# Two sequence layers on one core: every fourth low part of the weights is subtracted by GpSimd

## The chip, the cores and the metric

One core of a Trainium2 chip runs the whole kernel. The time is the device time in microseconds (us); before and after are compared by medians of several runs. A profiled execution gives the trace from which all rows below come. The engines are TensorE (PE, its weight loads as PEld), VectorE (DVE), ScalarE (ACT), GpSimd (POOL) and SyncE (SP), which here only issues transfers.

## The reference

Two layers are computed for 256 tokens of width 2048, in float32, the first one's output (after a norm) feeding the second.

```python
h = _rmsnorm(x, norm_gain);  u = h @ w_in            # first layer
o_a = fox attention (8 heads of 128) * silu(z_a)     # causal softmax with forget gates
o_b = rwkv7 scan (16 heads of 64), group norm, * silu(z_b)
m = sigmoid(g_a) * (o_a @ w_proj_fox) + sigmoid(g_b) * (o_b @ w_proj_rwkv)
x = _rmsnorm(x + m @ w_out, final_norm_gain)
...
proj = rms_norm(x, norm_g) @ w_in                    # second layer
o_conv = (gated causal convolution) @ w_conv_out
o_mla  = (latent attention, 16 heads, rope) @ w_mla_out
o_mem  = (attention to 256 memory tokens) @ w_mem_out
x = x + (sigmoid(g_conv)*o_conv + sigmoid(g_mla)*o_mla + sigmoid(g_mem)*o_mem) @ w_o
```

Nearly all arithmetic is the product of 256 tokens with some 84 million weights.

## The kernel before, in words

The weights lie in memory packed into 658 blocks of 128 x 1024 floats, in the order in which the matrix products (`gemm`) use them. TensorE multiplies in a float32 form of lower precision (`F32R`), so each operand is split into a high part (a copy in that form) and a low part (the operand less its high part), and each product is three matmuls: high by high, high by low, low by high.

`conv_to` prepares a block. `dma_to` loads it into a `raw` buffer (SP's queue, L402); ScalarE copies it to `whi` (`acopy`, L278 in the profile); VectorE subtracts that from `raw` to give `wlo` (`sub`, which goes through the helper `tt`, L241). There are four buffers each of `raw`, `whi` and `wlo` (`NRAW`, `NHI`), and `gemm` asks for blocks three ahead of the one that it multiplies (`AHEAD`). `wlo` of a block must be done before its `raw` buffer is loaded again; `whi` and `wlo` of a block must be read by TensorE before the block four later is written there. Block i = 0 is done in two halves; the first twelve blocks are taken in an order of their own (`block_at`).

All else (norms, attention, the scan, splitting activations, moving results out) is written as "side jobs": Python generators whose steps `pump` issues between the matmuls of `gemm`. A planner decides how many. It keeps a clock for TensorE, VectorE and ScalarE; each helper (`mm`, `tt`, `ts`, `stt`, `act`) adds the cost that it expects of its instruction, `CD + n / 960` us for `tt`. `busy()` stops the issue of steps while VectorE's or ScalarE's clock is more than a margin (1.5 us) ahead of TensorE's, and a step is not followed by the next one of its job before the result is expected. `finish` issues what is left of a job at once, where a later product needs it. The written order gives priorities; the framework then lays down the order in each engine's queue by when it expects an instruction's inputs, so that fills or loads with free buffers can stand far ahead of their place in the text. On each engine the queue is then run in order.

GpSimd's queue holds, before the change, only fills and the issue of transfers: in `head_rs` (L663 to L665: a row of norms to memory, `hd`, and back spread over partitions, `hr`), in `rwkv_job` (L879, L995 `Ld`, L1002 to L1006, L1020 to L1027 `Xd`, `Yd`, `XA`, `YF`), in `conv_job` (L1546 to L1550), and loads of `mt`, `fg`, `xr`, `xbd`, `xo`.

Of the kernel before, what the change touches and what calls it, by code (L numbers as in the profile page):

```python
# [10 lines left out]
F32 = mybir.dt.float32  # L11
# [3 lines left out]
ALU = mybir.AluOpType  # L15
# [211 lines left out]
def hybrid_kernel(ctx: ExitStack, tc: tile.TileContext, io, out):  # L227
    nc = tc.nc
# [10 lines left out]
    def tt(o, a, b, op):  # L239
        clock["dve"] += CD + fsz(o) / 960.0  # L240
        DVE.tensor_tensor(out=o, in0=a, in1=b, op=op)  # L241
# [7 lines left out]
    def sub(o, a, b):  # L249
        tt(o, a, b, ALU.subtract)  # L250
# [29 lines left out]
    def acopy(o, a, scale=1.0):  # L280
        act(o, a, AF.Copy, scale=scale)
# [18 lines left out]
    def nm(s):  # L300
        serial[0] += 1
        return f"{s}_{serial[0]}"
# [69 lines left out]
    groups, nblk = weight_groups()  # L372
    byname = {e["name"]: e for e in groups}
    st = {"dma": 0, "conv": 0}
    raw_t, hi_t, lo_t = {}, {}, {}

    def block_at(i):

        if i >= 12:
            return i  # L380
        return 4 + 2 * (i // 3) + i % 3 - 1 if i % 3 else i // 3

    def half(p):
        return slice(512 * p, 512 * p + 512)

    def dma_to(n):
        while st["dma"] < min(n, nblk):
            i = st["dma"]
            j = block_at(i)
            raw_t[j] = wpool.tile([128, 1024], F32, name=nm("raw"), tag="raw", bufs=NRAW)  # L390
            x = i // 3
            if i == 0:
                for p in range(2):
                    nc.scalar.dma_start(out=xt[0][:, 2 * p:2 * p + 2, :], in_=io["xT"][:, 2 * p:2 * p + 2, :])
                    nc.sync.dma_start(out=raw_t[j][:, half(p)], in_=io["W"][j, :, half(p)])
            else:
                if i % 3 == 0 and x < 4:
                    nc.sync.dma_start(out=xt[x], in_=io["xT"][:, 4 * x:4 * x + 4, :])
                if i == 12:
                    nc.sync.dma_start(out=lw2f[0:96, :], in_=io["w2"])  # L400
                    nc.sync.dma_start(out=la2f[0:96, :], in_=io["a2"])
                nc.sync.dma_start(out=raw_t[j], in_=io["W"][j])  # L402
            st["dma"] += 1

    def conv_to(n):
        while st["conv"] < min(n, nblk):
            i = st["conv"]
            j = block_at(i)
            dma_to(i + 1)
            hi_t[j] = wpool.tile([128, 1024], F32R, name=nm("whi"), tag="hi", bufs=NHI)  # L410
            lo_t[j] = wpool.tile([128, 1024], F32R, name=nm("wlo"), tag="lo", bufs=NHI)
            for p in ([half(0), half(1)] if i == 0 else [slice(0, 1024)]):
                acopy(hi_t[j][:, p], raw_t[j][:, p])
                sub(lo_t[j][:, p], raw_t[j][:, p], hi_t[j][:, p].bitcast(F32))
            del raw_t[j]
            st["conv"] += 1
            dma_to(i + 1 + NRAW)
# [60 lines left out]
    def gemm(name, pairs, evac):  # L478
# [5 lines left out]
        for b0 in range(0, e["nb"], step):  # L484
            bl = list(range(base + b0, base + min(b0 + step, e["nb"])))
            conv_to(bl[-1] + 1)
            conv_to(bl[-1] + 1 + AHEAD)
            ks = [(b, i, (b - base) * per + i) for b in bl for i in range(per)]
            if acc is None:
# [119 lines left out]
    def out_pair(name):  # L609
        return tuple(claim(t) for t in new_pair(name))  # L610
# [107 lines left out]
    def start_tile(i):  # L718

        x = xt[i]  # L720
        p = new_pair("xg")
        xg.append(p)
        for cs in ((range(2), range(2, 4)) if i == 0 else (range(4),)):
            for c in cs:
                acopy(p[0][:, c, :], x[:, c, :], scale=pc("norm_gain", 4 * i + c))
            for c in cs:
                stt(p[1][:, c, :], x[:, c, :], pc("norm_gain", 4 * i + c), p[0].bitcast(F32)[:, c, :], ALU.mult,
                    ALU.subtract)
            if cs[0] == 0:
                conv_to(3 * i + 1)  # L730
# [1026 lines left out]
    for j in range(4):  # L1757
        p = out_pair("ol")
# [10 lines left out]
    for j in range(4):  # L1769
        gemm(f"gl{j}", h2, gate(gt))  # L1770
        p = out_pair("mg")
# [68 lines left out]
```

## Time and profile before

| | |
|---|---|
| median of 3 runs | 2010.94 us (2008.88 to 2014.69) |
| the profiled execution | 2012.98 us, its span 2011.2 us |
| granted TensorE clock | 0.998 |
| busy in the span | TensorE 1996.2, VectorE 1276.6, ScalarE 985.3, GpSimd 61.5 us |
| weights converted | 659 high parts and 659 low parts (658 blocks, one in halves) |
| moved by transfers | 370.86 MB |

How to read it: the span runs from the first to the last instruction. A row of groups gives line, engine and operation, result and operands with their shapes, how often, the busy time and the mean in ns, and the idle time of that engine just ahead, with what ended it. A row of waits gives who waited for whom, the total, how often, and the longest. A row of the timeline gives start and duration in us. Ends of matmuls are modelled, so a busy TensorE may hide short gaps.

### The profile page before, as it was taken

Reading aid. Unit: us, or ns where it says so; the run is one execution under the profiler, and the core shown is the slowest. Engines: PE = TensorE matmul, PEld = TensorE weight load, DVE = VectorE, ACT = ScalarE, POOL = GpSimd, SP = SyncE. Lnnn points to the kernel's source line nnn. Section 1 sums busy time; section 2 is a strip of 40 time slices with the busy share of each in tenths; the row PEclk is TensorE's granted clock in tenths of the full one; section 3 lists DMA queues with packets and bytes.
Section 4 is the critical chain, followed back from the end, with each engine's and each line's share of the span. In section 5 each row is a group of like instructions: output and inputs, shape, how many; then the busy total and the mean of one; then the engine's idle time right before and its main releaser. Section 6 shows DMA issues by size and latency. Waiting matters only on the chain.

```text
span 2011.2 us, 30300 instructions
## 1 busy us (share of the span) xinstructions
PE 1996.2 (99%) x11916; PEld 1736.4 (86%) x11916; DVE 1276.6 (63%) x2039; ACT 985.3 (49%) x1344; POOL 61.5 (3%) x112
## 2 busy tenths in 40 slices
PE   9999999999999999999999999999999999999999
PEld 9999999898877888888898888888888889988887
DVE  8776846878447578666756766657556555555554
ACT  6744445454444545455545545445445444444442
POOL 0002000020100000000000000000000000000000
PEclk9999999999999999999999999999999999999999
DMA  7455544536546766665555554655555555666564
GB/s 271 159 183 162 193 141 138 171 114 202 180 156 223 230 197 203 201 219 190 181 189 184 168 177 154 206 181 191 169 178 188 168 179 179 189 213 212 190 199 146
DMA packets 104190, 370.86 MB, mean 184 GB/s; under 512 B 12466, under 2 KB 13410, under 8 KB 104048
## 3 DMA queue, kind: packets, MB, share of 16 engines
q1 hardware_dynamic: 97136, 350.11, 53.0%
q0 software_dynamic: 6480, 18.21, 3.2%
q8 instruction: 93, 1.52, 0.3%
q10 hardware_dynamic: 432, 0.61, 0.1%
q14 instruction: 49, 0.40, 0.1%
HBM read 361.00 MB, written 5.80 MB: 182 GB/s over the span
## 4 chain that ended last, share of the span: by engine, by line
PE 96%; DVE 2%; DMA 1%; issue 1%; ACT 0%; POOL 0%; SPq 0%; DVEq 0%; POOLq 0%
PE acc.lz L286 5%; PE acc.ga L286 4%; PE acc.gc L286 4%; PE acc.gm L286 4%; PE acc.gl L286 4%; PE acc.wo L286 4%; PE acc.w L286 4%; PE acc.lo L286 4%; PE acc.gb L286 4%; PE acc.fq L286 2%; PE acc.r L286 2%; PE acc.mz L286 2%; PE acc.fk L286 2%; PE acc.zb L286 2%; PE acc.pf L286 2%; PE acc.vr L286 2%
## 5 line engine op out<-in xcount | busy, mean ns | idle before, releaser
L241 DVE TENSOR_TENSOR wlo<-raw,whi 128x1024 fp32r<-128x1024 f32 (+1 forms) x659 | 804.0, 1223 | 615.8 <-ACT whi L278 607.8
L278 ACT ACTIVATE whi<-raw 128x1024 fp32r<-128x1024 f32 (+1 forms) x659 | 696.1, 1058 | 800.9 <-PE acc.lo L286 51.1
L286 PE MATMUL acc.lz<-h2l,whi 128*128 128x256 f32 x256 | 72.3, 283 | 0.0
L286 PE MATMUL acc.lz<-h2h,whi 128*128 128x256 f32 x256 | 72.3, 283 | 0.0
L286 PE MATMUL acc.lz<-h2h,wlo 128*128 128x256 f32 x256 | 72.0, 283 | 0.0
L286 PE MATMUL acc.gb<-wlo,hh 128*128 128x512 f32 x128 | 49.9, 390 | 1.7 <-DVE wlo L241 1.7
L286 PE MATMUL acc.ga<-whi,hl 128*128 128x512 f32 x128 | 50.4, 394 | 0.0
L286 PE MATMUL acc.ga<-wlo,hh 128*128 128x512 f32 x128 | 50.3, 393 | 0.0
L286 PE MATMUL acc.gc<-whi,h2h 128*128 128x512 f32 x128 | 50.2, 393 | 0.0
L286 PE MATMUL acc.gm<-whi,h2h 128*128 128x512 f32 x128 | 50.1, 392 | 0.0
L286 PE MATMUL acc.gl<-wlo,h2h 128*128 128x512 f32 x128 | 50.1, 391 | 0.0
L286 PE MATMUL acc.gm<-whi,h2l 128*128 128x512 f32 x128 | 50.0, 391 | 0.0
L286 PE MATMUL acc.gc<-wlo,h2h 128*128 128x512 f32 x128 | 50.0, 391 | 0.0
L286 PE MATMUL acc.gm<-wlo,h2h 128*128 128x512 f32 x128 | 50.0, 391 | 0.0
L286 PE MATMUL acc.gc<-whi,h2l 128*128 128x512 f32 x128 | 50.0, 390 | 0.0
L286 PE MATMUL acc.ga<-whi,hh 128*128 128x512 f32 x128 | 50.0, 392 | 0.0
L286 PE MATMUL acc.gl<-whi,h2h 128*128 128x512 f32 x128 | 49.9, 391 | 0.0
L286 PE MATMUL acc.w<-wlo,mgh 128*128 128x512 f32 x128 | 49.9, 390 | 0.0
L286 PE MATMUL acc.wo<-wlo,mh 128*128 128x512 f32 x128 | 49.9, 390 | 0.0
L286 PE MATMUL acc.w<-whi,mgh 128*128 128x512 f32 x128 | 49.9, 390 | 0.0
L286 PE MATMUL acc.gl<-whi,h2l 128*128 128x512 f32 x128 | 49.8, 389 | 0.0
L286 PE MATMUL acc.wo<-whi,ml 128*128 128x512 f32 x128 | 49.8, 389 | 0.0
(646 smaller groups left out, 5533.1 us busy)
## 6 DMA issues: line engine op xcount, KB each, us to landing
raw<-in_W SPq DMA_DIRECT2D x657, 512.0 KB, 3.4
hr<-hd POOLq DMA_DIRECT2D x8, 256.0 KB, 4.5
xr<-in_xtm POOLq DMA_DIRECT2D x4, 512.0 KB, 6.1
mt<-in_memT POOLq DMA_DIRECT2D x4, 512.0 KB, 6.5
xbd<-x1g POOLq DMA_DIRECT2D x4, 512.0 KB, 3.7
xo<-xbd POOLq DMA_DIRECT2D x4, 512.0 KB, 4.9
out_tm<-xo SPq DMA_DIRECT2D x8, 256.0 KB, 4.8
xt<-in_xT SPq DMA_DIRECT2D x3, 512.0 KB, 7.6
```

The lines of the kernel that those rows point to most:

```text
L241: DVE.tensor_tensor(out=o, in0=a, in1=b, op=op)
L278: ACT.activation(out=o, in_=a, func=f, scale=scale, **kw)
L286: TE.matmul(o, lhsT=l, rhs=r, start=start, stop=stop)
```

## The change

In `conv_to`, for each block whose number i (in order of conversion) leaves 3 when divided by 4, and which is not among the last 8, the low part is computed by GpSimd's `tensor_tensor` instead of VectorE's. These are 162 of 658 blocks. The operands, the buffers and the place in the text are the same. The helper `sub` is not called for them, so that the planner's VectorE clock is not advanced either, and the planner has no clock for GpSimd.

```diff
             for p in ([half(0), half(1)] if i == 0 else [slice(0, 1024)]):
                 acopy(hi_t[j][:, p], raw_t[j][:, p])
-                sub(lo_t[j][:, p], raw_t[j][:, p], hi_t[j][:, p].bitcast(F32))
+                if i % 4 == 3 and i < nblk - 8:
+                    nc.gpsimd.tensor_tensor(out=lo_t[j][:, p], in0=raw_t[j][:, p], in1=hi_t[j][:, p].bitcast(F32), op=ALU.subtract)
+                else:
+                    sub(lo_t[j][:, p], raw_t[j][:, p], hi_t[j][:, p].bitcast(F32))
             del raw_t[j]
             st["conv"] += 1
             dma_to(i + 1 + NRAW)
```

## The prediction

> **What bounds the kernel now.** I read the page's head first, then TensorE's own waits, then the two groups that make the weights, then one quiet stretch as a timeline, and last everything that GpSimd does.
>
> ```profile
> span 2011.2 us, 30300 instructions
> PE 1996.2 (99%) x11916; PEld 1736.4 (86%) x11916; DVE 1276.6 (63%) x2039; ACT 985.3 (49%) x1344; POOL 61.5 (3%) x112
> PE 96%; DVE 2%; DMA 1%; issue 1%; ACT 0%; POOL 0%; SPq 0%; DVEq 0%; POOLq 0%
> ...
> L241 DVE TENSOR_TENSOR wlo<-raw,whi 128x1024 fp32r<-128x1024 f32 (+1 forms) x659 | 804.0, 1223 | 615.8 <-ACT whi L278 607.8
> ```
>
> TensorE is busy for 1996.2 of 2011.2 us, so 15.0 us are all that any change to another engine could win by those records. VectorE has the low parts as its largest group, 804.0 of its 1276.6 us, and 37% of the span free. The second view, TensorE's waits, says how much of the 15.0 us the low parts cause:
>
> ```profile
> PE acc.vr L286 <- DVE wlo L241: 2.6, 1, 2.6
> PE lora L286 <- ACT xgh L278: 1.7, 1, 1.7
> PE acc.gb L286 <- DVE wlo L241: 1.7, 1, 1.7
> PE acc.fz L286 <- DVE wlo L241: 1.5, 2, 1.0
> PE acc.zb L286 <- DVE wlo L241: 1.1, 2, 0.9
> ```
>
> Four places, 2.6 + 1.7 + 1.5 + 1.1 = 6.9 us, is the whole price of late low parts: 0.34% of the time.
>
> Third, a quiet stretch, as ScalarE (high part), VectorE (low part) and the weight queue do it:
>
> ```profile
> 1858.25 1.06 ACT L278 ACTIVATE whi<-raw 128x1024 fp32r<-128x1024 f32 x1 [1.66 <-PE acc.lo L286]
> 1860.97 1.06 ACT L278 ACTIVATE whi<-raw 128x1024 fp32r<-128x1024 f32 x1 [1.66 <-PE acc.lo L286]
> ...
> 1869.13 1.06 ACT L278 ACTIVATE whi<-raw 128x1024 fp32r<-128x1024 f32 x1 [1.66 <-PE acc.lo L286]
> 1859.35 1.23 DVE L241 TENSOR_TENSOR wlo<-raw,whi 128x1024 fp32r<-128x1024 f32 x1 [1.50 <-ACT whi L278]
> 1860.60 22.09 SPq L402 DMA_DIRECT2D raw<-in_W  x9
> raw<-in_W SPq DMA_DIRECT2D x657, 512.0 KB, 3.4
> ```
>
> The period is 1860.97 - 1858.25 = 2.72 us a block. A high part starts when TensorE has left the block four before it (four buffers), so TensorE still has three blocks, 8.16 us, until it needs this one. The low part is done 1860.58 - 1858.25 = 2.33 us after that start: 5.8 us early. At its end the queue reloads the raw buffer (1860.60, landing 3.4 us later), which is converted four blocks on, at 1869.13; the reload is 1869.13 - 1860.60 - 3.4 = 5.1 us early. These two spares carry the forecast.
>
> **The change, part by part.** The weights have 658 blocks; those with i % 4 == 3 below 650 are i = 3, 7, ... 647, 162 of them. One such low part comes up every 4 x 2.72 = 10.9 us.
>
> *VectorE loses 162 x 1.223 = 198 us.* That is worth something only where TensorE waits for it, the 6.9 us. One block in four moves, and the others stay behind the same VectorE work, so I take a quarter: -1.7 us (ends: 0 and -6.9).
>
> *GpSimd gains 162 subtractions of 128x1024.* No such operation is in the trace. The nearest rows, fills on the same engine:
>
> ```profile
> 199.30 1.23 DVE L241 TENSOR_TENSOR wlo<-raw,whi 128x1024 fp32r<-128x1024 f32 x1 [1.66 <-ACT whi L278]
> 198.96 0.97 POOL L1003 MEMSET W<- 64x1024 f32 x1
> 199.85 0.98 POOL L1006 MEMSET YF<- 128x1024 f32 x1
> ```
>
> A fill writes one stream of 1024 in 0.98 us; a subtraction reads two and writes one. Lower end 0.98 (all three overlap), upper end 3 x 0.98 = 2.94 (none do). I take the upper end, since no row shows a read beside a write on that engine. The low part is then ready 1.10 + 2.94 = 4.04 us after its high part's start, 4.1 us early for TensorE; the reload is issued 1.7 us later than now and still lands 3.4 us early. So in quiet stretches the cost is 0.
>
> From where would it not be 0? Four raw buffers and every fourth block: the moved blocks all use the same raw buffer. High part to subtraction (1.10), subtraction T, reload (3.4), next high part must fit in 10.9 us: T may be 6.4 us. Beyond that, each further us is paid 162 times.
>
> *Beside VectorE.* The rows above show a fill and a VectorE subtraction overlapping with neither longer (0.97 and 0.98, 1.23). But a fill only writes. [...] I take no loss from overlap in the sum and put the loss in the first rival.
>
> *The start.* Here there are no three blocks of lead:
>
> ```profile
> 14.17 1.05 ACT L278 ACTIVATE whi<-raw 128x1024 fp32r<-128x1024 f32 x1
> 15.37 1.23 DVE L241 TENSOR_TENSOR wlo<-raw,whi 128x1024 fp32r<-128x1024 f32 x1
> 18.04 0.28 PE L286 MATMUL lora<-xgh,wlo 128*128 128x256 f32 x1
> ```
>
> This is the block i = 3. Its low part is ready at 16.60 and read at 18.04. On GpSimd it would be ready at 15.3 + 2.94 = 18.2, 0.2 us late. For i = 3, 7 and 11 together I write +1 us (ends: 0, where VectorE's relief pays it back, and 3 x 1.7 = +5).
>
> *GpSimd's queue.* The change's words are not quite so: that queue does hold steps of side jobs, their DMA issues and fills, and some wait in it:
>
> ```profile
> L663 POOL DMA_DIRECT2D hd<-hy x4 | 2.4, 596 | 276.1 <-DVE hy L241 142.1 <-DVE gate L603 104.3 <-DVE mx L1191 29.8
> L1024 POOL DMA_DIRECT2D XA<-Xd x4 | 2.7, 680 | 3.9 <-DMA Xd<-W 3.9
> 619.98 0.56 POOL L663 DMA_DIRECT2D hd<-hy  x1 [104.27 <-DVE gate L603]
> 624.47 1.28 POOL L665 DMA_DIRECT2D hr<-hd  x2 [3.94 <-DMA hd<-hy]
> 511.79 1.35 POOL L1024 DMA_DIRECT2D XA<-Xd  x2 [3.48 <-DMA Xd<-W]
> 513.13 2.57 POOL L1027 DMA_DIRECT2D YF<-Yd  x4
> ```
>
> The 104 us were mere idleness, as an engine with little to do shows them. The 3.94 us are a real head-of-queue wait: a low part behind it comes 3.94 + 1.28 = 5.2 us late, against 4.1 spare: 1.1 us of TensorE. Behind the XA issues: 3.48 + 1.35 + 2.57 = 7.4, or 3.3 us. There are four of the first kind (hd x4) and two of the second (XA x4, issued in pairs). A moved block comes every 10.9 us and these stretches are 5 to 7 us long, so about half are hit: (4 x 1.1 + 2 x 3.3) / 2 = 5.5 us if every hit has the longest wait; queue order is fixed beforehand by expected readiness, so most subtractions are placed ahead of such an issue, and I take +1 (ends 0, +11). The other way round, a side job's DMA issue stands up to 2.94 us behind a subtraction; VectorE's own wait for such data is what made the gb wait:
>
> ```profile
> 629.84 1.67 DVE L261 SCALAR_TENSOR_TENSOR CE<-CE,par,hr 128x256 f32<-128x256 f32 x4 [3.64 <-DMA hr<-hd]
> 631.43 1.22 DVE L241 TENSOR_TENSOR wlo<-raw,whi 128x1024 fp32r<-128x1024 f32 x1
> ```
>
> GpSimd will be busy 162 x 2.94 = 476 us, 24%, so the mean delay of an issue is 0.24 x 1.5 = 0.4 us, on four such chains: +1 us.
>
> *The weight queue* (SP) holds the reload of a moved block 1.7 us longer; the next reload waits for a low part ending 2.72 us after the present one, so it is not held up.
>
> *The planner.* `sub` also advanced the planner's VectorE clock by 0.15 + 1024/960 = 1.22 us; the direct call does not. In VectorE-bound stretches `pump` now issues side-job steps sooner, so the written order changes everywhere. TensorE's work stays the same. I take 0, with ends -8 (15.0 idle less 6.9 counted above) and +8.
>
> Sum: 2012.98 (the profiled execution; span 2011.2 and 1.8 around it) - 1.7 + 1 + 1 + 1 + 0 = 2014.3. That execution stands 2.0 above the median 2010.94, so against the median: 2012.
>
> **The rivals.** 0.3%, 6 us, is about what a measurement of this kernel tells from no change: same is 2004.9 to 2017.0.
>
> First, slower: *VectorE and GpSimd keep each other from reading.* The place is where VectorE is dense:
>
> ```profile
> 50.00:75.00 25.00, 25.00 (x197) 24.55 (x196) 22.84 (x40) 17.37 (x25) 1.08 (x2) 1.00 0.53 177
> 225.00:250.00 25.00, 25.00 (x125) 21.24 (x124) 21.73 (x41) 11.67 (x16) 0.60 (x2) 1.00 0.58 197
> 350.00:375.00 25.00, 25.00 (x136) 21.61 (x135) 22.11 (x42) 12.78 (x18) 0.00 (x0) 1.00 0.56 177
> 450.00:500.00 50.00, 50.00 (x285) 44.09 (x284) 45.02 (x91) 25.41 (x33) 0.00 (x0) 1.00 0.60 194
> 750.00:800.00 50.00, 50.00 (x226) 41.41 (x225) 42.86 (x62) 26.85 (x34) 1.08 (x2) 1.00 0.63 202
> sum 175.00, PE 175.00 PEld 152.90 DVE 154.56 ACT 94.08 POOL 2.76; mean PE 35.00 PEld 30.58 DVE 30.91 ACT 18.82 POOL 0.55
> ```
>
> (columns: span, then PE, PEld, DVE, ACT, POOL busy). In these 175 us fall 16 moved blocks; VectorE keeps 154.6 - 16 x 1.22 = 135 us. If the two take turns, 135 + 16 x 2.94 = 182 of 175: 7 us too much, 2019. If GpSimd gets only VectorE's gaps, T = 2.94 / 0.23 = 12.8 us there, over the 6.4 that the raw buffer allows: 16 x 6.4 = 102, 2114 at worst. Elsewhere VectorE is about half busy and T = 5.9, still inside. It decides from T = 6.4 us. For it: the low parts read two tensors; against it: the fills show nothing. Chance 0.22, most of it between 2017 and 2035.
>
> Second, slower: *head-of-queue waits on GpSimd* hit at their longest, +11 - 1 more: 2022. Against it, the 4.1 us spare. Chance 0.08.
>
> [...] Chance 0.06.
>
> Fourth, faster: the 6.9 us go entirely, because VectorE's relief lets its side jobs end before they collide, and the start costs nothing: 2010.94 - 6.9 = 2004. It needs all four places cured by moving one block in four, or a luckier order. Chance 0.18. That the change does nothing measurable is the forecast itself: 0.46, with its own range 2006 to 2017.
>
> **How the numbers follow.** Faster 0.18, same 0.46, slower 0.22 + 0.08 + 0.06 = 0.36. Low 2003 leaves out about 0.06 of the fast side; high 2035 leaves out about 0.1, the part of the first rival in which GpSimd gets only gaps for long.
>
> **What would show it.** In the profile after: 162 subtractions on POOL with a mean of 1 to 3 us (over 6.4 proves me wrong); VectorE's subtractions still 1223 ns (longer: the first rival); TensorE's waits on POOL low parts of a few us at the start and behind hr and XA issues, and its old 6.9 us of waits on VectorE down to about 5; ScalarE's waits for the raw DMA not grown; the first subtraction as long as the later ones. A span over 2020 with TensorE waiting on VectorE would point to the planner's order, which I set at 0.

## The result and the profile after

| | before | after |
|---|---|---|
| median of the runs | 2010.94 us | 2028.55 us (2026.83 to 2028.71, 3 runs) |
| ratio to before, 95% interval | | 1.0082 [1.0069, 1.0096] |
| profiled execution, span | 2012.98, 2011.2 us | 2028.71, 2026.9 us |

The change costs some 17 us. From the head of the profiled page of after and its groups:

```profile
span 2026.9 us, 30281 instructions
PE 2001.2 (99%) x11916; PEld 1740.0 (86%) x11916; DVE 1196.8 (59%) x1877; ACT 982.9 (48%) x1344; POOL 459.0 (23%) x274
...
L241 DVE TENSOR_TENSOR wlo<-raw,whi 128x1024 fp32r<-128x1024 f32 (+1 forms) x497 | 620.0, 1251 | 629.0 <-ACT whi L278 626.0 <-PE acc.zb L286 1.7
L415 POOL TENSOR_TENSOR wlo<-raw,whi 128x1024 fp32r<-128x1024 f32 x162 | 397.3, 2453 | 1419.5 <-ACT whi L278 1419.4
```

The 162 subtractions are on GpSimd, at 2453 ns each. VectorE is busy 79.8 us less, not 198: what it still does has become longer. By the trace, 65 of its steps beside a GpSimd subtraction are longer than the same step was before (against its median there, by more than 0.15 us), by 112 us together. TensorE is idle for 2026.9 - 2001.2 = 25.7 us (before 15.0, so +10.7), and busy for 5.0 us more with the same 11916 matmuls. These two, 10.7 + 5.0, are the whole difference of the spans. TensorE's longest waits in after:

```profile
PE acc.fz L286 <- DVE wlo L241: 5.5, 2, 4.1
PE acc.vr L286 <- DVE wlo L241: 5.0, 1, 5.0
PE u L286 <- DMA XA<-Xd: 4.0, 3, 1.7
```

No wait in the whole list is for a low part made by GpSimd. TensorE waits for low parts that *VectorE* still makes, and for side jobs (XA). Two of the four old waits are gone (gb, zb: 2.8 us), the other two (vr, fz: 4.1 us) have become 10.5. The stretch of 20 to 640 us before, then that and the rest, 640 to 2000 us, after (columns: span, then PE, PEld, DVE, ACT, POOL busy, granted clock, DMA share, GB/s):

```profile
20.00:640.00 620.00, 612.12 (x4975) 560.04 (x4975) 430.82 (x752) 302.25 (x445) 43.83 (x75) 1.00 0.53 167
```

```profile
20.00:640.00 620.00, 601.10 (x4906) 550.98 (x4905) 426.39 (x714) 296.40 (x439) 157.92 (x121) 0.99 0.50 164
640.00:2000.00 1360.00, 1359.26 (x6808) 1154.10 (x6807) 746.70 (x1123) 665.19 (x876) 298.40 (x148) 1.00 0.57 191
```

Nearly all the idle time that came on top lies ahead of 640 us, in the first layer's side jobs: TensorE is idle there for 18.9 us instead of 7.9. Behind it, where two thirds of the moved subtractions are, it is idle for 0.7 us.

**What is late, step by step.** VectorE and GpSimd after, around the first rwkv job's transfer `hr`:

```profile
124.14 0.48 DVE L261 SCALAR_TENSOR_TENSOR r<-acc.r,par,r 128x255 f32<-128x255 f32 x1 [0.36 <-ACT r L278]
124.54 1.96 DVE L241 TENSOR_TENSOR hy<-hy,ht 128x256 f32<-128x256 f32 x1
137.81 1.23 DVE L241 TENSOR_TENSOR KK<-KK,hr 128x1024 f32<-128x1024 f32 x1 [4.21 <-DMA hr<-hd]
145.03 4.83 DVE L241 TENSOR_TENSOR BK<-KK,IP 64x512 f32<-64x512 f32 x4
151.18 1.22 DVE L241 TENSOR_TENSOR wlo<-raw,whi 128x1024 fp32r<-128x1024 f32 x1
123.83 2.40 POOL L415 TENSOR_TENSOR wlo<-raw,whi 128x1024 fp32r<-128x1024 f32 x1 [10.07 <-ACT whi L278]
129.99 1.30 POOL L668 DMA_DIRECT2D hr<-hd  x2 [2.45 <-DMA hd<-hy]
146.87 2.45 POOL L415 TENSOR_TENSOR wlo<-raw,whi 128x1024 fp32r<-128x1024 f32 x1 [9.12 <-ACT whi L278]
```

And the same steps before:

```profile
124.94 0.43 DVE L241 TENSOR_TENSOR hy<-hy,ht 128x256 f32<-128x256 f32 x1
128.03 1.29 POOL L665 DMA_DIRECT2D hr<-hd  x2 [1.65 <-ACT whi L278]
135.18 1.22 DVE L241 TENSOR_TENSOR KK<-KK,hr 128x1024 f32<-128x1024 f32 x1 [2.79 <-DMA hr<-hd]
143.41 2.78 DVE L241 TENSOR_TENSOR BK<-KK,IP 64x512 f32<-64x512 f32 x4
147.51 1.23 DVE L241 TENSOR_TENSOR wlo<-raw,whi 128x1024 fp32r<-128x1024 f32 x1
```

GpSimd subtracts from 123.83 to 126.23. `hy`, which began at 124.54, ends at 126.50 and took 1.96 us instead of 0.43: it stood until the subtraction was done. The `r` step between them, which reads its first tensor in TensorE's accumulator (`acc.r`), ran its 0.48 us undisturbed inside the same subtraction. So `hy` ends 1.13 us later than before. The issue of `hr` is then 1.96 us late (129.99 for 128.03) and KK 2.63 us (137.81 for 135.18); what goes beyond the 1.13 is in the transfers between them (`hd` lands 2.88 us after its issue instead of 1.79, the second `hr` 7.07 instead of 6.41). At BK 1.62 us of this are left (145.03 for 143.41), and by then another moved block comes up: one of the four BK steps stands behind the subtraction of 146.87, which adds 2.05 us (4.83 for 2.78). The next low part, the one that TensorE waits for, begins at 151.18 instead of 147.51, 3.67 us late. The wait of 2.6 us at vr became 5.0.

At fz, in the second rwkv job, the last step ahead of the awaited low part (397.46) is again a held one. AV has one tensor as operand and a scalar for each partition:

```profile
393.91 2.44 POOL L415 TENSOR_TENSOR wlo<-raw,whi 128x1024 fp32r<-128x1024 f32 x1 [12.41 <-ACT whi L278]
394.14 3.32 DVE L257 TENSOR_SCALAR AV<-TA,ka,oka 128x256 f32<-128x256 f32 x4
...
395.96 1.38 DVE L257 TENSOR_SCALAR AV<-TA,ka,oka 128x256 f32<-128x256 f32 x4
```

(the last row is before's). These are 1.94 of the 4.1 us of that wait. Earlier in the same chain `hr` is issued sooner than before (375.02 for 377.39), yet it lands later (384.01 for 382.58): there it is the transfer that is longer, not a step on VectorE. That is so in general; the median from issue to landing, before, then after:

```profile
hr<-hd POOLq DMA_DIRECT2D x8, 256.0 KB, 4.5
hr<-hd POOLq DMA_DIRECT2D x8, 256.0 KB, 5.6
```

It is 5.6 to 5.8 us in the four kernels here in which GpSimd subtracts the 53 moved blocks ahead of 640 us, and 4.1 to 5.0 in the eight others. `xbd`, which GpSimd issues in the second half, takes 5.6 to 6.0 us where it subtracts the later blocks and 3.5 to 3.9 elsewhere. So transfers that GpSimd issues land later where it also subtracts; by what, and how much of the loss this is, was not tested.

A GpSimd instruction can be the one that stands, too. This subtraction took 4.19 us for 2.40; VectorE's `wlo` of 625.32, with its usual 1.21 us, lies within it:

```profile
624.96 4.19 POOL L415 TENSOR_TENSOR wlo<-raw,whi 128x1024 fp32r<-128x1024 f32 x1 [6.56 <-ACT whi L278]
```

**The 5.0 us of longer matmuls** are for the larger part a lower granted clock. The stretches at half clock, first before, with the 3.4 us ahead of it, then after (the clock is the third number from the end):

```profile
438.00:441.40 3.40, 2.30 (x17) 1.80 (x16) 2.78 (x10) 0.79 (x3) 3.17 (x6) 1.00 0.14 24
441.50:444.90 3.40, 3.40 (x16) 3.22 (x15) 1.43 (x4) 2.29 (x7) 1.58 (x3) 0.50 0.11 19
```

```profile
150.20:157.00 6.80, 4.54 (x21) 4.55 (x22) 6.75 (x14) 0.00 (x0) 0.00 (x0) 0.50 0.42 154
399.40:402.80 3.40, 3.40 (x18) 3.40 (x17) 3.37 (x7) 0.00 (x0) 0.00 (x0) 0.50 0.75 253
515.40:522.20 6.80, 5.79 (x71) 4.92 (x72) 1.43 (x1) 2.11 (x3) 0.33 (x1) 0.50 0.56 161
```

Behind the first 20 us, up to TensorE's last matmul, these are all. In the first 20 us after has none and before has one:

```profile
8.00:11.40 3.40, 3.40 (x18) 3.40 (x17) 2.35 (x4) 3.40 (x5) 0.00 (x0) 0.50 1.03 406
```

TensorE is busy in them for 3.40 + 3.40 = 6.80 us before and for 4.54 + 3.40 + 5.79 = 13.73 us after. What the lower clock makes of the same matmul shows at vr, first at 0.50, then at 1.00:

```profile
153.05 0.41 PE L286 MATMUL acc.vr<-hl,whi 128*128 128x256 f32 x1
153.26 0.41 PE L286 MATMUL acc.vr<-hh,wlo 128*128 128x256 f32 x1
157.20 0.28 PE L286 MATMUL acc.vr<-hl,whi 128*128 128x256 f32 x1
157.32 0.28 PE L286 MATMUL acc.vr<-hh,wlo 128*128 128x256 f32 x1
```

They begin 0.21 us apart instead of 0.12. If all work in these stretches is longer by that ratio, the difference costs (13.73 - 6.80) x (1 - 0.12 / 0.21) = 3.0 us, an estimate; what the rest of the 5.0 is was not taken apart.

The first stretch of after begins within the wait of 5.0 us at vr, the second behind the one of 4.1 at fz. The length of a wait alone does not say whether the clock falls. At the same place, vr, the wait of 2.6 us before left it at 1.00, and so did one of 3.0 us in the kernel with five blocks below; one of 2.1 us in the kernel with one fill each was followed by half (those two kernels in this order):

```profile
149.00:153.00 4.00, 3.78 (x31) 3.78 (x32) 4.00 (x8) 0.00 (x0) 0.00 (x0) 1.00 0.52 157
148.30:151.30 3.00, 3.00 (x14) 3.00 (x15) 3.00 (x6) 0.00 (x0) 0.00 (x0) 0.50 0.54 175
```

Ahead of the stretch of before at 441.50 TensorE is idle for 3.40 - 2.30 = 1.10 us in 3.40. What decides is not shown here.

### The profile page after: what moved, and what is told of

Same layout as the page of the kernel before. It is cut to its first block, busy times and chain, and to the rows that moved or that the text cites. A ratio compares the mean times of both kernels' runs of the same rounds, so it can differ in the third digit from the quotient of the medians.

```text
span 2026.9 us, 30281 instructions
## 1 busy us (share of the span) xinstructions
PE 2001.2 (99%) x11916; PEld 1740.0 (86%) x11916; DVE 1196.8 (59%) x1877; ACT 982.9 (48%) x1344; POOL 459.0 (23%) x274
## 4 chain that ended last, share of the span: by engine, by line
PE 91%; DVE 5%; DMA 2%; issue 1%; ACT 1%; SPq 0%; POOL 0%; DVEq 0%; ACTq 0%
PE acc.lz L286 5%; PE acc.gc L286 4%; PE acc.gm L286 4%; PE acc.gl L286 4%; PE acc.w L286 4%; PE acc.lo L286 4%; PE acc.gb L286 4%; PE acc.wo L286 3%; PE acc.ga L286 3%; PE acc.fq L286 2%; PE acc.vr L286 2%; PE acc.mz L286 2%; PE acc.cu L286 2%; PE acc.cb L286 2%; PE acc.cz L286 2%; PE acc.mk L286 2%
## 5 line engine op out<-in xcount | busy, mean ns | idle before, releaser
L241 DVE TENSOR_TENSOR wlo<-raw,whi 128x1024 fp32r<-128x1024 f32 (+1 forms) x497 | 620.0, 1251 | 629.0 <-ACT whi L278 626.0
L415 POOL TENSOR_TENSOR wlo<-raw,whi 128x1024 fp32r<-128x1024 f32 x162 | 397.3, 2453 | 1419.5 <-ACT whi L278 1419.4
L241 DVE TENSOR_TENSOR W<-W,W 64x31 f32<-64x31 f32 (+15 forms) x124 | 57.3, 462 | 3.8 <-DMA W<-Ld 0.6
```

The source lines that it names most:

```text
L415: nc.gpsimd.tensor_tensor(out=lo_t[j][:, p], in0=raw_t[j][:, p], in1=hi_t[j][:, p].bitcast(F32), op=ALU.subtract)
```

## The experiments

The theory: a GpSimd instruction that reads keeps VectorE instructions on operands in SBUF (the on-chip memory for tensors) standing until it ends (the *hold*), and this costs where VectorE is dense and a chain of a side job runs through it. Rivals: the written *order*, since the planner's clock is no longer advanced for 162 blocks; GpSimd's *queue*, in which side jobs' issues now stand behind subtractions; and a small cost per subtraction wherever it stands. The last two columns split the change of the span as above: time in which TensorE is idle, and time by which it is busy longer. They are of one profiled execution of each kernel, against that of before, so that they need not add up to the difference of the medians. The edits are against the kernel after, where it is not said otherwise.

| kernel | median us | before on the same chip | ratio [95%] | idle | busy |
|---|---|---|---|---|---|
| planner alone | 2020.63 | 2012.34 | 1.0043 [1.0031, 1.0055] | +2.0 | +4.3 |
| GpSimd, clock kept | 2034.24 | 2012.34 | 1.0111 [1.0098, 1.0124] | +12.1 | +9.9 |
| the first 53 blocks alone, clock kept | 2035.76 | 2012.39 | 1.0114 [1.0098, 1.0130] | +11.4 | +9.8 |
| the last 109 alone | 2012.91 | 2011.87 | 1.0003 [0.9994, 1.0012] | -0.8 | -0.1 |
| one copy each | 2029.49 | 2011.87 | 1.0077 [1.0063, 1.0091] | +9.4 | +9.3 |
| one fill each | 2019.10 | 2012.39 | 1.0035 [1.0021, 1.0049] | +2.9 | +2.1 |
| two fills each | 2018.36 | 2012.34 | 1.0032 [1.0020, 1.0044] | +1.5 | +3.0 |
| four quarters each | 2029.12 | 2012.34 | 1.0085 [1.0073, 1.0097] | +10.5 | +9.8 |
| dearer clock | 2016.67 | 2011.87 | 1.0021 [1.0012, 1.0030] | -0.7 | +3.1 |
| five blocks | 2014.97 | 2011.87 | 1.0010 [1.0001, 1.0018] | +0.2 | -0.7 |

**Order against engine.** First the planner alone: VectorE makes all low parts, but the planner's clock is not advanced for the 162.

```diff
-                    nc.gpsimd.tensor_tensor(out=lo_t[j][:, p], ...)
+                    DVE.tensor_tensor(out=lo_t[j][:, p], ...)
```

> All 658 low parts on VectorE; the 162 chosen ones are issued without advancing the planner's VectorE clock, so the written order is nearly that of the changed kernel. Lock theory (a VectorE instruction with two SBUF inputs, or one from SBUF to SBUF in tensor_scalar form, that starts beside a GpSimd subtraction waits for its end): nothing to wait for, so 2008 to 2015, the 0.3% around before. Order theory (the planner issues side-job steps too early and VectorE falls behind): the loss is here too, 2020 to 2035, and more than after, since VectorE isn't relieved. Queue theory (GpSimd's occupation holds up side-job transfers): 2008 to 2015.

Then the engine alone: GpSimd subtracts, and the clock is advanced as before, so that the written order is that of before. The order in the queues is not quite: the framework lays it down by expected readiness, and TensorE's matmuls run in another order from the 159th on.

```diff
                     nc.gpsimd.tensor_tensor(out=lo_t[j][:, p], ...)
+                    clock["dve"] += CD + 1024 / 960.0
```

> The 162 low parts on GpSimd, and the planner's VectorE clock advanced by the same 1.22 us as before, so the written order is nearly that of before. Lock theory: the loss stays, 2020 to 2030, with VectorE low parts up to 3.6 us long and the wait for hr or the BK products showing on TensorE. Order theory: the loss goes, 2008 to 2014. Queue theory: the loss stays, 2020 to 2030, but with VectorE's instructions at their usual length.

Measured: 8 us for the order alone, where the hold alone would have cost nothing, and 22 us for GpSimd with the order kept, 4 above the highest time that was expected of the hold. The order's loss shows as waits for side jobs that before did not have, with VectorE's subtractions at their 1222 ns:

```profile
PE bon L286 <- ACT rrh L278: 4.2, 1, 4.2
```

With GpSimd and the old order, the waits are again for VectorE's low part at vr and for the side jobs:

```profile
PE u L286 <- DMA XA<-Xd: 6.3, 3, 4.3
PE acc.vr L286 <- DVE wlo L241: 4.9, 1, 4.9
```

The two parts do not add: 8 + 22 is 30, and both together cost 17. By the planner's own intent that is plausible, since with the clock not advanced it fills the VectorE time that was set free; why the remainder is just 17 was not taken apart.

**Place.** GpSimd takes only the moved blocks before i = 212, with the clock kept, or only those behind it, as in the change.

```diff
-                if i % 4 == 3 and i < nblk - 8:
+                if i % 4 == 3 and i < 212:
```

```diff
-                if i % 4 == 3 and i < nblk - 8:
+                if i % 4 == 3 and 212 <= i < nblk - 8:
```

> GpSimd subtracts only the moved blocks before i = 212 (53 of them), with the planner's clock advanced, so in the order of before. Theory A (all the loss is made where VectorE has little room and side jobs are due): the whole loss of the 162 in that order, 2030 to 2037 us. Rival B (the late subtractions have a share in it in proportion to their number): 53/162 of 22 us, 2017 to 2022 us.

> GpSimd subtracts only the moved blocks from i = 215 on (109 of the 162), behind the gb group, where the trace after lost nothing. Theory A (VectorE instructions held behind a subtraction, which costs only where VectorE has no room and a side job's result is due): the same subtractions of about 2.4 us, some VectorE instructions again held to 2.4 us or more, no TensorE wait on them above 2 us, 2009 to 2015 us. Rival B (each moved subtraction costs a little wherever it stands: 17 us over 162 is 0.11 us each): 109 x 0.11 = 12 us more, 2021 to 2026 us.

The 53 early ones cost what all 162 cost in that order (1.0114 against 1.0111), the 109 late ones nothing, though they last about as long (2441 ns in the mean, the early ones 2541). That excludes a price per subtraction. In the early kernel the largest wait is for XA, behind a chain of small VectorE steps on `W`; one of them, beside the subtraction of 234.61, took 2.60 us, its neighbours 0.41.

**Kind.** VectorE makes all low parts; at the 162 places GpSimd first writes the low part's tile, which VectorE then overwrites: once as a copy of raw (reads and writes), once as a fill (writes only). Against the kernel before:

```diff
+                if i % 4 == 3 and i < nblk - 8:
+                    nc.gpsimd.tensor_copy(lo_t[j][:, p], raw_t[j][:, p])
                 sub(lo_t[j][:, p], ...)
```

```diff
+                if i % 4 == 3 and i < nblk - 8:
+                    nc.gpsimd.memset(lo_t[j][:, p].bitcast(F32), 0.0)
                 sub(lo_t[j][:, p], ...)
```

> VectorE subtracts all; at the 162 places GpSimd copies raw into the low part's tile first (one tensor read, one written) and VectorE overwrites it. Theory A (only a GpSimd instruction with two tensors to read holds VectorE): VectorE's subtraction keeps its mean of 1222 to 1226 ns and none of its instructions beside a copy is held, as beside the fills; VectorE waits for the copies as it did for the fills, so 2016 to 2023 us. Rival B (any GpSimd instruction that reads holds it): mean of 1235 ns or more, instructions beside a copy that end with it, 2024 to 2040 us.

> The pair of the copies: at the same 162 places GpSimd fills the low part's tile with zeros (writes only) instead of copying raw into it; VectorE then subtracts as before, and waits for the fill as it waited for the copy. Theory A (it is GpSimd's reading that holds VectorE): no VectorE instruction is held, mean of the subtraction 1222 to 1225 ns, 2010 to 2016 us. Rival B (what cost in the copies was GpSimd's time, its queue or VectorE's wait for it, which a fill of 0.96 us has in common with a copy of 1.05): 2023 to 2032 us.

The copies first:

```profile
L241 DVE TENSOR_TENSOR wlo<-raw,whi 128x1024 fp32r<-128x1024 f32 (+1 forms) x659 | 801.6, 1228 | 554.2 <-ACT whi L278 538.6 <-POOL wlo L415 9.5 <-PE acc.vr L286 2.9
L415 POOL CAST wlo<-raw 128x1024 fp32r<-128x1024 f32 x162 | 194.8, 1203 | 1608.3 <-PE acc.gc L286 86.5 <-PE acc.gm L286 85.7 <-PE acc.lz L286 82.9
1005.84 0.15 DVE L241 TENSOR_TENSOR tn<-tn 128x2 f32<-128x2 f32 x1
1006.23 0.95 DVE L241 TENSOR_TENSOR tn<-tn 128x2 f32<-128x2 f32 x1
1006.12 1.04 POOL L415 CAST wlo<-raw 128x1024 fp32r<-128x1024 f32 x1 [9.87 <-PE acc.mq L286]
```

Then the fills:

```profile
L241 DVE TENSOR_TENSOR wlo<-raw,whi 128x1024 fp32r<-128x1024 f32 (+1 forms) x659 | 803.8, 1223 | 611.8 <-ACT whi L278 559.7 <-POOL wlo L415 37.5 <-issue 8.6
L415 POOL MEMSET wlo<- 128x1024 f32 x162 | 155.0, 957 | 1641.0 <-PE acc.gm L286 88.7 <-PE acc.gc L286 87.3 <-PE acc.lz L286 84.4
227.31 1.31 DVE L241 TENSOR_TENSOR W<-W,W 64x255 f32<-64x255 f32 x3
228.10 0.95 POOL L415 MEMSET wlo<- 128x1024 f32 x1 [10.57 <-PE acc.fk L286]
55.62 0.96 POOL L415 MEMSET wlo<- 128x1024 f32 x1 [10.56 <-PE acc.kr L286]
55.79 0.93 DVE L255 TENSOR_SCALAR mn<-fx 8x256 f32<-8x256 f32 x1
...
55.81 0.27 DVE L255 TENSOR_SCALAR mn<-fx 8x256 f32<-8x256 f32 x1
```

(the last row is before's).

Beside a copy, a step on two elements a partition takes 0.95 us instead of 0.15 and ends with the copy. Beside a fill, the third `W` step, which has two tensors as operands, takes its usual 0.42. So the narrow form of the theory fell: not only an instruction with two tensors to read holds VectorE; one that reads a single tensor does too. (The mean of VectorE's subtractions beside the copies, 1228 ns, lies between the two expectations.)

A fill is not without a hold, though. The step `mn`, with one tensor and a scalar, takes 0.93 us instead of 0.27 beside a fill and ends just behind it. By the trace this is a matter of VectorE's step: of those that began within a fill and would have ended within it, all 9 of this kind (`TENSOR_SCALAR`) stood until its end, and none of the 19 `TENSOR_TENSOR` steps did; beside the subtractions of the change 9 of 10 and 29 of 46 stood. The others there read an accumulator of TensorE's, or were ahead, so that the subtraction stood.

The copies cost 17.6 us, the fills 6.7, though VectorE waited longer for the fills (37.5 us against 9.5). The fills also missed their expectation of 2010 to 2016 us, by 3. What these 7 us are was not shown: the held scalar steps, VectorE's waits for the fills and another order in the queues are all in that kernel, and so the 11 us between the two kernels are not shown to be the reading alone.

Two fills in place of one:

```diff
+                if i % 4 == 3 and i < nblk - 8:
+                    for _ in range(2):
+                        nc.gpsimd.memset(lo_t[j][:, p].bitcast(F32), 0.0)
                 sub(lo_t[j][:, p], ...)
```

> All low parts on VectorE with its clock advanced; GpSimd fills the same 162 low-part tiles twice with zeros ahead of the subtraction (2 x 0.98 = 1.95 us of its queue each time, writing and never reading). Lock theory, if it is about reading: VectorE's instructions keep their usual length (low part 1.22 us mean) and the time is 2008 to 2016. Lock theory, if writes hold it as well: 2018 to 2030. Queue theory: GpSimd's queue is as occupied (80% of it) as in the changed kernel, so 2018 to 2028. Order theory: 2008 to 2014.

GpSimd is then busy for 311 us with them, 1.6 times as long as with the copies (194.8), and VectorE waits 181.9 us for them; still they cost 6 us against 17.6 (2 us more than was expected of fills that hold nothing):

```profile
L416 POOL MEMSET wlo<- 128x1024 f32 x324 | 311.2, 960 | 1504.9 <-PE acc.gm L286 80.6 <-PE acc.gc L286 78.9 <-PE acc.lz L286 76.3
```

GpSimd's time and its queue as such are therefore not what the copies cost beyond some 6 us.

**A shorter hold?** Each subtraction in four pieces of 128x256. If a hold is as long as the piece that causes it, a part of the loss should come back.

```diff
-                    nc.gpsimd.tensor_tensor(out=lo_t[j][:, p], ...)
+                    for q in range(4):
+                        c = slice(256 * q, 256 * q + 256)
+                        nc.gpsimd.tensor_tensor(out=lo_t[j][:, c], ...)
```

> The changed kernel, but each of the 162 subtractions cut into four of 128x256 (each about 0.65 us). [...] Order theory: nothing changes, 2025 to 2031. Queue theory: the occupation is the same or longer, 2025 to 2035.

```profile
L241 DVE TENSOR_TENSOR wlo<-raw,whi 128x1024 fp32r<-128x1024 f32 x495 | 631.2, 1278 | 646.3 <-ACT whi L278 645.0
L417 POOL TENSOR_TENSOR wlo<-raw,whi 128x256 fp32r<-128x256 f32 x648 | 507.6, 815 | 1326.0 <-ACT whi L278 1321.2 <-PE acc.r L286 4.7
```

The time is the same (1.0085 against 1.0082), so nothing of the loss came back. VectorE does step in between the pieces: by the trace 174 of its steps are held, by 0.5 us in the mean, instead of 65 by 1.7, and it is busy for 1178.4 us, 18.4 less than in the change. But four pieces take 4 x 815 = 3260 ns instead of 2453, VectorE's own subtractions are longer than in the change (1278 for 1251), and TensorE's wait at vr is 5.4 us, no shorter. Why the shorter holds bring nothing was not taken apart.

**The order the other way.** The kernel before, with the planner's share of each VectorE instruction at 0.18 us, so that it holds side jobs back.

```diff
-CD, CA, PEF = 0.15, 0.17, 0.0133
+CD, CA, PEF = 0.18, 0.17, 0.0133
```

> The kernel before with the planner's fixed share of every VectorE instruction at 0.18 instead of 0.15 us: nothing moves to GpSimd, side jobs are written a little later instead of earlier. Theory A (written earlier, steps of side jobs stand ahead of low parts that TensorE needs): no loss, 2004 to 2013 us. Rival B (the order before was a lucky one, and any other loses some 8 us): 2015 to 2024 us, with TensorE waits of 2 us or more at places where before had none.

It lost 4 to 5 us (1.0021), with its longest wait where before had 1.1:

```profile
PE acc.zb L286 <- DVE wlo L241: 3.6, 1, 3.6
```

So the idea that only an earlier order loses fell. Both neighbours of the order before are worse, one by 4 to 5 and one by 8 us. A new order alone can thus cost that much, and the queues of every kernel here are in a somewhat different one.

**The five blocks that were late.** GpSimd takes only the blocks for which TensorE waited before, with the clock kept.

```diff
-                if i % 4 == 3 and i < nblk - 8:
+                if i in (45, 112, 113, 185, 186):
...
+                    clock["dve"] += CD + 1024 / 960.0
```

> GpSimd subtracts only the five blocks for which TensorE waited on VectorE in the trace before (i = 45, 112, 113, 185, 186), the planner's clock advanced as before, so the written order stays. Theory A (those 6.9 us are VectorE's queue alone, and five subtractions hold little): the four waits go, 2004 to 2009 us. Rival B (a held VectorE instruction stands ahead of the next low part, so the wait moves one block on): a wait of 1.5 us or more at the neighbour, 2010 to 2015 us.

```profile
PE acc.vr L286 <- DVE wlo L241: 3.0, 1, 3.0
PE acc.zb L286 <- DVE wlo L241: 2.1, 2, 1.9
...
L416 POOL TENSOR_TENSOR wlo<-raw,whi 128x1024 fp32r<-128x1024 f32 x5 | 14.8, 2978 | 15.5 <-ACT whi L278 15.5
139.87 4.12 POOL L416 TENSOR_TENSOR wlo<-raw,whi 128x1024 fp32r<-128x1024 f32 x1 [10.61 <-ACT whi L278]
```

Nothing is won (1.0010). gb's wait is gone, fz's is about what it was (1.8 for 1.5, a third of it for a low part of GpSimd's), those of vr and zb now go to a VectorE low part beside the moved one and are longer (3.0 for 2.6, 2.1 for 1.1), and the subtractions, 2978 ns in the mean and up to 4.12 us, are themselves held where VectorE is dense. No version here beats the kernel before.

## Why the prediction was right and wrong

The measured 2028.55 us lies within the range, but the likeliest case, no measurable change at 2012, did not come. The first rival did, and with it a term of the sum that was set at nothing. The range held because it had been drawn up to 2035 for that rival, not because the sum was right.

- *Beside VectorE, "no loss from overlap in the sum"*: this is the step that failed. It was 0, and the kernel with the clock kept lost 22 us. At TensorE's two longest waits the holds are in the rows above (BK 2.05 us, AV 1.94); how much of the 22 is later transfers or another order in the queues stays open. The evidence offered for 0, two fills beside a subtraction, was a true reading of the wrong kind: beside a fill a step with two tensors took its usual time (`W`, 0.42 us), beside a copy or a subtraction it did not (`tn`, 0.95 us for 0.15; `hy`, 1.96 for 0.43).
- *The first rival* named the mechanism, and four of its five dense windows lie where the loss was; the fifth, 750 to 800 us, lost nothing. Its price "take turns" counted work against room over whole windows: 7 us too much, 2019. What costs is not the sum of the work but which instruction stands: `hy`, then BK, and AV at fz, in chains that TensorE waits for. On top come later transfers and stretches at half clock. Its worse price, GpSimd left with gaps only and T over 6.4 us, did not come: 2.45 us in the mean, 4.19 in the row above.
- *The planner, "I take 0", ends -8 and +8*: measured +8 alone, at the upper end.
- *VectorE's relief, -1.7*: gb and zb were relieved by 2.8 us; vr and fz grew by more.
- *T, between 0.98 and 2.94*: 2.45, so the upper end was somewhat dear. The quiet stretches cost nothing, as the spares of 4.1 and 3.4 us said: TensorE's idle time behind 640 us is 0.7 us, and the last 109 alone give 1.0003.
- *The start, +1*: in the first 20 us TensorE is idle for 1.8 us instead of 2.8, so it cost nothing.
- *The first subtraction as long as the later ones*: so it was, and what had the chance of 0.06 did not come. The first took 2.43 us, against a mean of 2453 ns:

```profile
14.68 2.43 POOL L415 TENSOR_TENSOR wlo<-raw,whi 128x1024 fp32r<-128x1024 f32 x1 [14.23 <-ACT whi L278]
```

- *GpSimd's queue, +1 and +1*: TensorE never waits for a low part behind an issue. The issue of `hr` was 1.96 us late, but because `hy` was held on VectorE and `hd` landed later, not because it stood behind a subtraction. The second +1 was 4 x 0.4 = 1.6 by its own figures. What the term left out is that the transfers themselves take longer.
- *Not foreseen at all*: the half clock, 3.0 of the 15.7 us by the estimate above.
- Of the signs named to look for, "a span over 2020 with TensorE waiting on VectorE" came, and would have misled: it was to point to the planner's order, which alone makes 8 us. "VectorE's subtractions still 1223 ns" was the one that told: 1251 looks harmless, since the mean spreads a few held ones of up to 3.7 us over 497, and the steps of the side jobs are in other groups. ScalarE's waits for the raw transfers had not grown (20.4 us before, 19.6 after), as the prediction said.

## What to carry to other kernels

Work moved from VectorE to GpSimd is not simply set free where VectorE is dense: here VectorE was busy 79.8 us less, not 198, and steps of its own stood until a GpSimd instruction that reads had ended (`hy` 1.96 us for 0.43 beside a subtraction, `tn` 0.95 for 0.15 beside a copy). So price it by the chains that run through VectorE at that place, and by those through GpSimd's own transfers, and move only where VectorE has room and nothing is due. Before counting an overlap as free, look for a row of the same kind (reading beside reading). And when a kernel's order is computed from costs, change the cost and the engine in separate runs.

## What the runs showed of the hardware

- What stands and what runs. Beside GpSimd's subtractions, 29 of 46 of VectorE's `TENSOR_TENSOR` steps and 9 of 10 `TENSOR_SCALAR` steps stood until the subtraction ended (`hy` 1.96 us for 0.43, the four AV 3.32 for 1.38); the `r` step that reads the accumulator ran inside one in 0.48. Beside the fills, none of 19 `TENSOR_TENSOR` steps stood (`W`, 0.42 us) and all 9 `TENSOR_SCALAR` steps did (`mn`, 0.93 for 0.27). GpSimd's subtraction could itself be longer: 4.19 us beside VectorE steps that were ahead of it, and 4.12 in the kernel with five blocks, for 2.40.
- A small instruction was held for most of the other's length: two elements a partition, 0.95 us instead of 0.15 beside a copy of 1.04.
- Transfers issued by GpSimd landed later where it also subtracted (median from issue to landing: `hr` 5.6 us for 4.5, `xbd` 5.6 for 3.7); the cause is open.
- TensorE's clock was 0.50 for 4.5 us of work behind a wait of 5.0 us, with matmuls that began 0.21 us apart instead of 0.12. At one place it stayed at 1.00 behind waits of 2.6 and 3.0 us and was 0.50 behind one of 2.1, so these runs give no bound for the length of a wait.
